# FFN gate and up projections as seven products of quadrants, with the down projection as a phase of its own

## The chip, the cores and the metric

One core of a Trainium2 chip runs the whole program. The time is device time in microseconds (us), lower is better. TensorE (PE) does the matmuls; VectorE (DVE), ScalarE (ACT) and GpSimd (POOL) do the element-wise work; SyncE (SP) issues the DMA transfers. Each engine works through its own list of instructions in a fixed order and waits where an operand is not there.

## The reference

The input is 1024 tokens of width 1024. Two attention layers (the first block) are followed by a second block, in which a SwiGLU feed-forward network stands at both ends of a mixing part:

```python
def swiglu(x, w_gate, w_up, w_down):
    return (jax.nn.silu(x @ w_gate) * (x @ w_up)) @ w_down
...
        h = h + 0.5 * swiglu(rms_norm(h, ffn1_norm[i]), ffn1_w_gate[i], ffn1_w_up[i], ffn1_w_down[i])
...
        h = h + 0.5 * swiglu(rms_norm(h, ffn2_norm[i]), ffn2_w_gate[i], ffn2_w_up[i], ffn2_w_down[i])
```

d_ff is 2816, so w_gate and w_up are 1024x2816 and w_down is 2816x1024. The mixing part between them has neighbourhood attention and an S5 state-space branch with a scan along the tokens; a small gated projection (ple) ends the program.

## The kernel before

All is fp32. Each fp32 operand is split into a high part and a remainder (hi, lo, both of type fp32r), and `mm3` forms a product with three matmuls per 128 rows of the contraction: hi with hi, hi with lo, lo with hi. So nearly everything on PE comes in threes, at lines 194, 195 and 196. Weights come from DRAM into a raw tile (`wraw`, two buffers), `split_w` makes hi on POOL (L184) and lo on DVE or POOL (L186).

The second block runs in this order: `ffn` (FFN1), `ssm_in` and `mix` (with the scan), `attn_out` and `mix_out`, `ffn` again (FFN2), `ple`. `ffn` goes through 22 tiles of 128 columns of d_ff. For one tile, `gate` and `up` each make two halves of 512 tokens (24 matmuls of 512 columns each, into PSUM tags G and S); tanh on ACT and products on DVE give the hidden tile, split again into hh and hl. For every two hidden tiles `down` multiplies with w_down (`draw`, split into dhi and dlo) and adds 16 pieces of 128x512 from PSUM tag T into h with DVE (L967). h, the residual, stays in SBUF. One FFN has 2112 gate and up matmuls and 1056 down matmuls, all of 512 columns.

In FFN1 the generator `also` is stepped once per tile; it is `ssm_matrices`, which makes the matrices of the scan with some 770 DVE operations on 64 columns (tiles gu, gM, gC; the rest of its tiles is called gen) and writes them to DRAM as `ssm_win`. The scan loads them as `sw` (L1183).

A tile framework fixes every engine's order at build time from the program's priorities; nothing is reordered on the chip.

## Time and profile before

| | |
|---|---|
| median of 3 runs | 3594.66 us (3594.66 to 3599.98) |
| the profiled execution | 3596.7 us |
| its span, first to last instruction | 3594.9 us |
| PE busy | 3463.1 us, 96% |
| DVE, ACT, POOL busy | 59%, 30%, 24% |
| mean granted TensorE clock | 0.987 |
| FFN1, FFN2 | about 1200 to 1955 us, about 2745 to 3465 us |

Busy time counts an instruction from its start to its end, and matmuls overlap their successors, so the pitch from start to start says what one costs. The granted clock is 1.00 at 2.4 GHz and 0.50 at 1.2 GHz; a stretch in between holds some of both. Windows are given in us from the span's start.

### The profile page before, as it was taken

What the parts mean: (1) busy time and instruction counts of PE and PEld (TensorE: products, weight loads), DVE (VectorE), ACT (ScalarE), POOL (GpSimd) and SP (SyncE); (2) the same over time, 40 slices, a digit from 0 to 9 for tenths busy, and PEclk for the clock granted to TensorE, in tenths of its full rate; (3) what the DMA queues carried; (4) which work ended last, traced back from release to release, by engine and by line L of the source; (5) the groups of instructions that cost most, each with busy time, mean ns of one, the idle gap of its engine ahead of it and who ended that gap; (6) DMA issues with size and microseconds to landing.
All of it is one profiled execution on the core that took longest, in us unless ns stands there. A gap on an engine that the chain in (4) does not pass through costs nothing. (4 is left out here: it accounts for less than half of the span.)

```text
span 3594.9 us, 53440 instructions
## 1 busy us (share of the span) xinstructions
PE 3463.1 (96%) x19400; PEld 3011.4 (84%) x19400; DVE 2108.4 (59%) x5436; ACT 1072.5 (30%) x2475; POOL 863.1 (24%) x970
## 2 busy tenths in 40 slices
PE   8999999999999999999999898998999999999998
PEld 7988899889889788888888786877798888888888
DVE  5656667646757966666544099428865444444465
ACT  3446645436745310000002310336611000000032
POOL 4233224323213311111112223343222101011112
PEclk9999999999999999999999999999999999999999
DMA  7567763657773222222212732577543111111113
GB/s 228 166 199 218 247 216 109 186 170 234 230 234 114 68 61 62 68 68 60 72 44 86 198 124 91 176 235 199 162 162 91 57 36 59 47 48 53 36 56 115
DMA packets 467671, 456.74 MB, mean 127 GB/s; under 512 B 45760, under 2 KB 354368, under 8 KB 467408
## 3 DMA queue, kind: packets, MB, share of 16 engines
q1 hardware_dynamic: 458192, 442.84, 40.9%
q10 hardware_dynamic: 9216, 10.49, 0.9%
q8 instruction: 154, 2.52, 0.3%
q14 instruction: 109, 0.89, 0.1%
HBM read 335.76 MB, written 117.41 MB: 126 GB/s over the span
## 5 line engine op out<-in xcount | busy, mean ns | idle before, releaser
L184 POOL TENSOR_SCALAR whi<-wraw 128x512 fp32r<-128x512 f32 (+1 forms) x460 | 297.3, 659 | 1903.1 <-PE G L195 837.9
L194 PE MATMUL G<-xh,whi 128*128 128x512 f32 x1472 | 583.9, 397 | 3.5 <-DVE slo L160 2.6
L196 PE MATMUL G<-xh,wlo 128*128 128x512 f32 x1472 | 578.6, 393 | 0.0
L195 PE MATMUL G<-xl,whi 128*128 128x512 f32 x1408 | 553.6, 393 | 0.2 <-DVE xl L157 0.2
L194 PE MATMUL G<-whi,xh 128*128 128x256 f32 (+1 forms) x1536 | 450.2, 293 | 10.2 <-DVE slo L157 5.8
L195 PE MATMUL G<-wlo,xh 128*128 128x256 f32 (+1 forms) x1536 | 444.2, 289 | 0.0
L967 DVE SCALAR_TENSOR_TENSOR h<-T,h 128x512 f32<-128x512 f32 x352 | 242.4, 689 | 333.8 <-PE T L196 331.5
L194 PEld LDWEIGHTS G<-xh,whi 128*128 128x128 f32 x1472 | 278.5, 189 | 62.3 <-DVE slo L160 2.9
L196 PEld LDWEIGHTS G<-xh,wlo 128*128 128x128 f32 x1472 | 277.9, 189 | 56.9
L195 PEld LDWEIGHTS G<-xl,whi 128*128 128x128 f32 x1408 | 266.3, 189 | 51.8 <-DVE xl L157 0.5
L194 PEld LDWEIGHTS G<-whi,xh 128*128 128x128 f32 x1536 | 296.7, 193 | 14.7 <-DVE slo L157 6.2
L195 PEld LDWEIGHTS G<-wlo,xh 128*128 128x128 f32 x1536 | 296.9, 193 | 1.0
L186 DVE TENSOR_TENSOR wlo<-wraw,whi 128x512 fp32r<-128x512 f32 x252 | 200.9, 811 | 118.4 <-POOL whi L184 118.3
L186 POOL TENSOR_TENSOR wlo<-wraw,whi 128x512 fp32r<-128x512 f32 (+1 forms) x208 | 267.8, 1301 | 4.7
L196 PE MATMUL G<-whi,xl 128*128 128x256 f32 (+1 forms) x896 | 262.8, 293 | 0.0
L194 PE MATMUL T<-dhi,hh 128*128 128x512 f32 x640 | 251.2, 393 | 0.0
L196 PE MATMUL T<-dhi,hl 128*128 128x512 f32 x640 | 249.4, 390 | 0.0
L195 PE MATMUL T<-dlo,hh 128*128 128x512 f32 x640 | 249.0, 389 | 0.0
L977 ACT ACTIVATE ft<-G 128x512 f32<-128x512 f32 x88 | 52.6, 597 | 579.9 <-PE G L196 579.8
L986 ACT ACTIVATE hh<-ft 128x512 fp32r<-128x512 f32 x88 | 54.5, 631 | 521.5 <-DVE ft L985 349.7
L194 PE MATMUL S<-xh,whi 128*128 128x512 f32 x512 | 200.2, 391 | 0.0
L196 PE MATMUL S<-xh,wlo 128*128 128x512 f32 x512 | 199.4, 390 | 0.0
(402 smaller groups left out, 7647.7 us busy)
## 6 DMA issues: line engine op xcount, KB each, us to landing
wraw<-w_in SPq DMA_DIRECT2D x144, 256.0 KB, 3.3
draw<-ffn_w_down SPq DMA_DIRECT2D x88, 256.0 KB, 2.6
wraw<-ffn_w_gate SPq DMA_DIRECT2D x86, 256.0 KB, 3.0
wraw<-ffn_w_up SPq DMA_DIRECT2D x86, 256.0 KB, 2.9
wraw<-w_out SPq DMA_DIRECT2D x64, 256.0 KB, 3.3
hk<-ka SPq DMA_DIRECT2D x48, 256.0 KB, 4.9
gs<-gt SPq DMA_DIRECT2D x32, 256.0 KB, 4.0
gl<-gs SPq DMA_DIRECT2D x32, 256.0 KB, 3.9
```

The source lines that it names most:

```text
L184: self.nc.gpsimd.tensor_scalar(hi, raw, 1.0, 0.0, op0=OP.mult, op1=OP.add)
L186: eng.tensor_tensor(lo, raw, f(hi), op=OP.subtract)
L194: t.matmul(out, lh, rh, start=first and i == 0, stop=False)
L195: t.matmul(out, lh, rl, start=False, stop=False)
L196: t.matmul(out, ll, rh, start=False, stop=last and i == n - 1)
L967: nc.vector.scalar_tensor_tensor(hs, ps, 0.25, hs, op0=OP.mult, op1=OP.add)
L977: nc.scalar.activation(t, pg, AF.Tanh, scale=0.5)
L986: nc.scalar.activation(hh[:, c], t, AF.Copy)
```

## The change

The activations x (tokens) and each weight are cut into quadrants. Instead of eight products of quadrants, seven products of sums are made (Strassen's scheme in Winograd's form): `ffn_up` takes 256 columns of gate or up at a time (11 steps, gate then up), and one product is 12 matmuls of 512 columns. The sums of x (s1 to s4) are made once in `halves_in` and `fourth`, mostly on POOL (L981, L983 and L989; these and the lines below are the changed kernel's); the sums of the weights (t1 to t4) are made on POOL (L1062 to L1065) for every step. `operand` splits each into hi (ACT) and lo (DVE, or POOL for w_down), in a ring of eight slots. The products are combined from PSUM on DVE (L1079 to L1092). The hidden tiles go to DRAM (`hid`, L1076).

`ffn_down` comes when all are done: for each half of the tokens and each half of the columns of w_down it accumulates four PSUM tiles over 22 steps k, 12 matmuls per step. In the first column half a hidden tile is loaded again (`hraw`, L1118) and split on ACT and DVE (L1120); w_down is loaded in both token halves. h comes from DRAM and goes there, in tiles hc and ht with two buffers each. `also` is stepped in this phase only, at every fourth k. Eight products (of j = 0 and 1) that need only the first half of the tokens are issued ahead of the rest.

Smaller edits: `weights` shifts tiles of 256 columns by 32 bytes; xn has one buffer in place of two; ple loads h from DRAM. Counted whole: 11 x 2 x 7 x 12 = 1848 gate and up matmuls per FFN in place of 2112, and 1056 down matmuls as before.

The core of the diff (the lines of `ffn` that go are in the listing above):

```diff
...
+    def weights(self, src, kt, n, pool=None, tag="w", bufs=4, raws=2, off=0):
+        o, size = off // 4, 1088 if pool is None else None
...
-            hi, lo = [self.T(pool, [128, 1088 if n == 352 else m * n], F32R, tag + x, bufs)[:, :m * n]
+            hi, lo = [self.T(pool, [128, size or m * n], F32R, tag + x, bufs)[:, o:o + m * n]
...
-        x = self.T(p, [128, 1024], F32, "xn", 2)
+        x = self.T(p, [128, 1024], F32, "xn", 1)
...
+    def halves_in(self, t, src, p, X, tag="T"):
...
+        sl = slice(t % 4 * 128, t % 4 * 128 + 128)
+        ps = []
+        for b in range(2):
+            ps.append(self.PS(tag, self.nT))
+            for j in range(4):
+                k = b * 4 + j
+                nc.tensor.transpose(ps[b][:, j * 128:j * 128 + 128], src[:, k * 128:k * 128 + 128], self.ident)
+            ps[b] = ps[b].rearrange("p (j n) -> p j n", j=4)
+        if t < 4:
+            hi, lo = X["a"]
+            for b in range(2):
+                self.split_ps(ps[b], hi[:, b * 4:b * 4 + 4, sl], lo[:, b * 4:b * 4 + 4, sl])
+            return
+        def tmp(n):
+            return self.T(p, [128, 4, 128], F32, n, 1)
+        def put(n, x):
+            hi, lo = [y[:, :, sl] for y in X[n]]
+            self.split_ps(x, hi, lo)
+        a21, a11, s1 = tmp("a21"), tmp("a11"), tmp("s1")
+        nc.scalar.activation(a21, ps[0], AF.Copy)
+        self.full(a11, X["a"], slice(0, 4), sl)
+        nc.vector.tensor_tensor(s1, ps[1], a21, op=OP.add)
+        put("b", ps[1])
+        put("s1", s1)
+        s2 = tmp("s2")
+        nc.gpsimd.tensor_tensor(s2, s1, a11, op=OP.subtract)
+        put("s2", s2)
+        nc.gpsimd.tensor_tensor(a21, a11, a21, op=OP.subtract)
+        put("s3", a21)
+        if "s4" in X:
+            self.fourth(sl, p, X, s2)
+    def full(self, dst, pair, k, sl):
+        self.nc.gpsimd.tensor_tensor(dst, f(pair[0])[:, k, sl], f(pair[1])[:, k, sl], op=OP.add)
+    def fourth(self, sl, p, X, s2=None):
+        a12 = self.T(p, [128, 4, 128], F32, "a11", 1)
+        self.full(a12, X["a"], slice(4, 8), sl)
+        if s2 is None:
+            s2 = self.T(p, [128, 4, 128], F32, "s2", 1)
+            self.full(s2, X["s2"], slice(0, 4), sl)
+        self.nc.vector.tensor_tensor(a12, a12, s2, op=OP.subtract)
+        hi, lo = [y[:, :, sl] for y in X["s4"]]
+        self.split_ps(a12, hi, lo)
+    def operand(self, src, lo_eng):
+        if not self.ring:
+            t = [self.T(self.wp, [128, 1024], F32R, x, 4) for x in ("whi", "wlo")]
+            self.ring = [[y[:, c:c + 512] for y in t] for c in (512, 0)]
+        hi, lo = self.ring.pop()
+        as_src = (lambda y: y.rearrange("p (k n) -> p k n", k=4)) if len(src.shape) == 3 else (lambda y: y)
+        self.nc.scalar.activation(as_src(hi), src, AF.Copy)
+        lo_eng.tensor_tensor(as_src(lo), src, as_src(f(hi)), op=OP.subtract)
+        return hi, lo
+    def ffn_up(self, X, wg, wu, hid, r, late, tags):
+        nc = self.nc
+        v = nc.vector
+        x = {n: [(hi[:, k], lo[:, k]) for k in range(4)] for n, (hi, lo) in X.items() if n != "a"}
+        x["a11"], x["a12"] = ([(X["a"][0][:, k], X["a"][1][:, k]) for k in range(b, b + 4)] for b in (0, 4))
+        turn = [0]
+        bufs = {"G": self.nG, "S": self.nS, "T": self.nT}
+        def product(W, n):
+            g = tags[turn[0] % len(tags)]
+            turn[0] += 1
+            ps = self.PS(g, bufs[g])
+            self.mm3(ps, self.four(W), x[n])
+            return ps
+        def tile(p, n, b):
+            return self.T(p, [128, 512], F32, n, b)
+        def first(w11, w21):
+            a = tile(r, "r1", 4)
+            nc.scalar.activation(a, product(w11(), "a11"), AF.Copy)
+            c = tile(r, "r2", 4)
+            v.tensor_tensor(c, a, product(w21(), "a12"), op=OP.add)
+            return a, c
+        def corner(src, j, k):
+            def get():
+                raw = self.T(self.wp, [128, 4, 128], F32, "wraw", 2)
+                nc.sync.dma_start(raw, src[k * 512:k * 512 + 512, j * 256:j * 256 + 128].rearrange("(k p) n -> p k n", p=128))
+                return self.operand(raw, v)
+            return get
+        early = {(j, i): first(corner(src, j, 0), corner(src, j, 1)) for j in range(2) for i, src in enumerate((wg, wu))}
+        p = late()
+        for j in range(11):
+            gates = {}
+            for i, src in enumerate((wg, wu)):
+                top, bot = [self.T(p, [128, 4, 256], F32, n, 2) for n in ("top", "bot")]
+                for k, y in enumerate((top, bot)):
+                    nc.sync.dma_start(y, src[k * 512:k * 512 + 512, j * 256:j * 256 + 256].rearrange("(k p) n -> p k n", p=128))
+                b11, b12, b21, b22 = top[:, :, 0:128], top[:, :, 128:256], bot[:, :, 0:128], bot[:, :, 128:256]
+                t1, t2, t3, t4 = [self.T(p, [128, 4, 128], F32, n, 1) for n in ("t1", "t2", "t3", "t4")]
+                if (j, i) in early:
+                    u, c11 = early[j, i]
+                else:
+                    u, c11 = first(lambda: self.operand(b11, v), lambda: self.operand(b21, v))
+                nc.gpsimd.tensor_tensor(t1, b12, b11, op=OP.subtract)
+                nc.gpsimd.tensor_tensor(t2, b22, t1, op=OP.subtract)
+                nc.gpsimd.tensor_tensor(t3, b22, b12, op=OP.subtract)
+                nc.gpsimd.tensor_tensor(t4, t2, b21, op=OP.subtract)
+                def done(c, hf, n):
+                    if i == 0:
+                        th = tile(p, "th", 2)
+                        nc.scalar.activation(th, c, AF.Tanh, scale=0.5)
+                        v.scalar_tensor_tensor(c, th, 1.0, c, op0=OP.add, op1=OP.mult)
+                        gates[hf, n] = c
+                    else:
+                        v.tensor_tensor(c, c, gates[hf, n], op=OP.mult)
+                        o = j * 256 + n * 128
+                        nc.sync.dma_start(hid[o:o + 128, hf * 512:hf * 512 + 512], c)
+                done(c11, 0, 0)
+                p6 = product(self.operand(t2, v), "s2")
+                v.tensor_tensor(u, u, p6, op=OP.add)
+                p7 = product(self.operand(t3, v), "s3")
+                u3 = tile(p, "r3", 2)
+                v.tensor_tensor(u3, u, p7, op=OP.add)
+                p5 = product(self.operand(t1, v), "s1")
+                c22 = tile(p, "r4", 2)
+                v.tensor_tensor(c22, u3, p5, op=OP.add)
+                v.tensor_tensor(u, u, p5, op=OP.add)
+                done(c22, 1, 1)
+                p3 = product(self.operand(b22, v), "s4")
+                v.tensor_tensor(u, u, p3, op=OP.add)
+                done(u, 0, 1)
+                p4 = product(self.operand(t4, v), "b")
+                v.tensor_tensor(u3, u3, p4, op=OP.subtract)
+                done(u3, 1, 0)
+    @staticmethod
+    def four(W):
+        return [(W[0][:, k * 128:k * 128 + 128], W[1][:, k * 128:k * 128 + 128]) for k in range(4)]
+    def ffn_down(self, hid, wd, src, dst, p, slots, then, also=None):
+        nc = self.nc
...
+        turn = 0
+        for hf in range(2):
+            H = slots(hf)
+            for c in range(2):
+                cs = slice(c * 512, c * 512 + 512)
+                acc = []
+                for t in range(4):
+                    g = "GS"[turn % 2]
+                    turn += 1
+                    acc.append(self.PS(g, self.nG if g == "G" else self.nS))
+                for k in range(22):
+                    hi, lo = H[k]
+                    if c == 0:
+                        raw = self.T(p, [128, 512], F32, "hraw", 3)
+                        nc.sync.dma_start(raw, hid[k * 128:k * 128 + 128, hf * 512:hf * 512 + 512])
+                        nc.scalar.activation(hi, raw, AF.Copy)
+                        nc.vector.tensor_tensor(lo, raw, f(hi), op=OP.subtract)
+                    raw = self.T(self.wp, [128, 512], F32, "wraw", 2)
+                    nc.sync.dma_start(raw, wd[k * 128:k * 128 + 128, cs])
+                    wh, wl = self.operand(raw, nc.gpsimd)
+                    for t in range(4):
+                        ts = slice(t * 128, t * 128 + 128)
+                        self.mm3(acc[t], [(hi[:, ts], lo[:, ts])], [(wh, wl)], k == 0, k == 21)
+                    if k % 4 == 3:
+                        next(also, None)
+                for t in range(4):
+                    rows = slice((hf * 4 + t) * 128, (hf * 4 + t) * 128 + 128)
+                    if c == 0:
+                        h = self.T(p, [128, 512], F32, "hc", 2)
+                        hc = h
+                    else:
+                        h = self.T(p, [128, 1024], F32, "ht", 2)
+                        nc.sync.dma_start(h[:, 0:512], dst[rows, 0:512])
+                        hc = h[:, cs]
+                    nc.sync.dma_start(hc, src[rows, cs])
+                    nc.vector.scalar_tensor_tensor(hc, acc[t], 0.25, hc, op0=OP.mult, op1=OP.add)
+                    nc.sync.dma_start(dst[rows, cs], hc)
+                    if c == 1:
+                        then(hf * 4 + t, h)
...
-            W = self.weights(self.I["w_out_2"][:, u * 256:u * 256 + 256], 8, 256)
+            W = self.weights(self.I["w_out_2"][:, u * 256:u * 256 + 256], 8, 256, off=32)
...
+                x = K.T(self.p, [128, 1024], F32, "xn", 1)
+                K.rms_tile(z, x, self.g)
+                K.halves_in(t, x, self.p, X)
...
+            def end(self):
+                self.X["s4"] = two(slot(K.big, "xl1"))
...
+                    K.fourth(slice(t * 128, t * 128 + 128), self.p, self.X)
...
+        self.ffn_up(nx.X, I["ffn1_w_gate_2"], I["ffn1_w_up_2"], hid, nx.r, late(nx.p, "late1"), "GSGSG")
...
+        self.ffn_down(hid, I["ffn1_w_down_2"], nx.hd, hd, p, places(nx.sx, p, ("xh0", "xl0"), ("xl1", "xh1"), ("sa", "sb", "sc"), 1), then, also())
...
+        self.ffn_up(X, I["ffn2_w_gate_2"], I["ffn2_w_up_2"], hid, r, late(p, "late2"), "GST")
...
+        self.ffn_down(hid, I["ffn2_w_down_2"], h2, h3, p, places(sx, p, ("xh0", "xh1"), ("xl0", "xl1"), ("sa", "sc", "sb")), then, also())
...
```

**At the entry of FFN1, PE.** Before, the last transposes of the normalized tokens (T<-ident) and what follows; the G and S rows are the first gate and up halves of the second 512 tokens.

```order
L195 MATMUL S_16548<-xl_3772_16072,whi_16452 128x512
L196 MATMUL S_16548<-xh_3771_16071,wlo_16453 128x512
L256 MATMUL T_16263<-ident,xn_16256 128x128 x4
L256 MATMUL T_16270<-ident,xn_16256 128x128 x4
L194 MATMUL G_16576<-xh_3793_16166,dhi_16386 128x512
L194 MATMUL S_16604<-xh_3793_16166,dhi_16396 128x512
L194 MATMUL G_16632<-xh_3793_16166,whi_16442 128x512
L194 MATMUL S_16660<-xh_3793_16166,whi_16452 128x512
```

After, at the same place; S_16561 is the first product that needs a sum of x (sb is the tile of s2) and a sum of weights.

```order
L196 MATMUL G_16524<-xh_3757_15875,whi_16501 128x512
L197 MATMUL G_16524<-sa_15876,whi_16501 128x512
L198 MATMUL G_16524<-xh_3757_15875,wlo_16502 128x512
L960 MATMUL T_16277<-ident,xn_16270 128x128 x4
L960 MATMUL T_16282<-ident,xn_16270 128x128 x4
L960 MATMUL T_16320<-ident,xn_16313 128x128 x4
L960 MATMUL T_16325<-ident,xn_16313 128x128 x4
L196 MATMUL S_16561<-sb_16178,whi_16557 128x512
L197 MATMUL S_16561<-sb_16178,whi_16557 128x512
L198 MATMUL S_16561<-sb_16178,wlo_16558 128x512
```

Before, products of plain weights follow the transposes; now a product of sums follows, and the ones of plain weights (G_16524) stand ahead of the transposes.

**At the same place, POOL.** Before: high parts of weights, and the layer norm and rstd of the last token tiles (h, rrs, lst).

```order
L539 TENSOR_TENSOR rrs_16138<-rrs_16138,mhalf 128x1
L690 TENSOR_TENSOR h<-h,lngb_14651 128x1024
L184 TENSOR_SCALAR whi_16452<-wraw_16454 128x512
L184 TENSOR_SCALAR whi_16452<-wraw_16458 128x512
L539 TENSOR_TENSOR rrs_16170<-rrs_16170,mhalf 128x1
L539 TENSOR_TENSOR lst_15940<-lst_15940,mhalf 128x1
L184 TENSOR_SCALAR whi_16819<-wraw_16821 128x512
L184 TENSOR_SCALAR whi_16819<-wraw_16825 128x512
L539 TENSOR_TENSOR rrs_16200<-rrs_16200,mhalf 128x1
L690 TENSOR_TENSOR h<-h,lngb_14651 128x1024
```

After, from the s2 of the last token tile to the sum t2 of the first weights:

```order
L981 TENSOR_TENSOR s_3840_16340<-s_3839_16332,a_3838_16331 128x512
L983 TENSOR_TENSOR a_3837_16330<-a_3838_16331,a_3837_16330 128x512
L989 TENSOR_TENSOR a_3842_16349<-xh_3757_15875,sa_15876 128x512
L989 TENSOR_TENSOR s_3843_16351<-sb_16178 128x512
L989 TENSOR_TENSOR s_3845_16358<-sb_16178 128x512
L989 TENSOR_TENSOR a_3844_16356<-xh_3757_15875,sa_15876 128x512
L989 TENSOR_TENSOR s_3847_16365<-sb_16178 128x512
L989 TENSOR_TENSOR a_3846_16363<-xh_3757_15875,sa_15876 128x512
L989 TENSOR_TENSOR s_3849_16372<-sb_16178 128x512
L989 TENSOR_TENSOR a_3848_16370<-xh_3757_15875,sa_15876 128x512
L1062 TENSOR_TENSOR t_3884_16546<-top_16542 128x512
L1063 TENSOR_TENSOR t_3885_16547<-bot_16543,t_3884_16546 128x512
```

Twelve additions of 128x512 stand between the last token tile and the first product of sums, where single high parts stood.

**In the middle of FFN1, DVE.** Before: gu, gM and gC are the scan's matrices; L967 adds into h, L985 makes the hidden tile, wlo is a low part of weights.

```order
L1046 TENSOR_TENSOR gu_3935_17274<-gM_17272,gen_16314 128x64
L967 SCALAR_TENSOR_TENSOR h<-T_17067,h 128x512
L1047 TENSOR_TENSOR gu_3936_17275<-gM_17272,gen_16315 128x64
L985 TENSOR_TENSOR ft_17196<-ft_17196,S_17227 128x512
L1048 TENSOR_TENSOR gM_17272<-gu_3935_17274,gu_3936_17275 128x4x16
L186 TENSOR_TENSOR wlo_17689<-wraw_17690,whi_17688 128x512
L1049 TENSOR_TENSOR gu_3935_17274<-gM_17272,gen_16314 128x64
L1050 TENSOR_TENSOR gu_3936_17275<-gM_17272,gen_16315 128x64
L186 TENSOR_TENSOR wlo_17689<-wraw_17694,whi_17688 128x512
L1051 TENSOR_TENSOR gM_17272<-gu_3935_17274,gu_3936_17275 128x4x16
```

After, in the down phase; hraw is a hidden tile that is loaded again, xl and so on its low part.

```order
L1173 TENSOR_TENSOR gM_20031<-gu_4491_20033,gu_4492_20034 128x4x16
L1120 TENSOR_TENSOR xl_4639_21298<-hraw_21331,xl_4639_21298 128x512
L1174 TENSOR_TENSOR gu_4491_20033<-gM_20031,gen_19750 128x64
L1175 TENSOR_TENSOR gu_4492_20034<-gM_20031,gen_19751 128x64
L1120 TENSOR_TENSOR xl_4639_21298<-hraw_21351,xl_4639_21298 128x512
L1176 TENSOR_TENSOR gM_20031<-gu_4491_20033,gu_4492_20034 128x4x16
L1171 TENSOR_TENSOR gu_4491_20033<-gM_20031,gen_19750 128x64
L1172 TENSOR_TENSOR gu_4492_20034<-gM_20031,gen_19751 128x64
L1120 TENSOR_TENSOR xl_4639_21298<-hraw_21373,xl_4639_21298 128x512
L1173 TENSOR_TENSOR gM_20031<-gu_4491_20033,gu_4492_20034 128x4x16
```

The same operations on matrices, which stood between all the FFN's other DVE work, now stand beside the hidden tiles of the down phase alone.

**From the products to the down phase, SP after the change.** The last stores of hidden tiles and the first loads.

```order
L1076 DMA hid_16377<-r_4425_19567 128x512
L1122 DMA wraw_19890<-ffn_w_down 128x512
L1076 DMA hid_16377<-r_4413_19475 128x512
L1076 DMA hid_16377<-r_4423_19550 128x512
L1122 DMA wraw_19944<-ffn_w_down 128x512
L1122 DMA wraw_19966<-ffn_w_down 128x512
L933 DMA rg_19615<-mix_norm 128x1024
L1118 DMA hraw_19635<-hid_16377 128x512
L1118 DMA hraw_19657<-hid_16377 128x512
L1118 DMA hraw_19677<-hid_16377 128x512
```

The first hidden tiles are loaded right behind the stores of the last ones; before the change there was no such place.

## Rows read from the trace of the kernel before

**Rows 1.** The page: busy time of each engine, share, instructions.

```profile
PE 3463.1 (96%) x19400; PEld 3011.4 (84%) x19400; DVE 2108.4 (59%) x5436; ACT 1072.5 (30%) x2475; POOL 863.1 (24%) x970
```

**Rows 2.** Windows of 600 us in FFN1 and FFN2.

```profile
core 0: us, PE busy (x) PEld busy (x) DVE busy (x) ACT busy (x) POOL busy (x), PEclk, DMA share, GB/s
1300.00:1900.00 600.00, 600.00 (x2725) 496.07 (x2724) 362.42 (x1010) 56.01 (x107) 74.54 (x122) 1.00 0.22 62
...
2800.00:3400.00 600.00, 600.00 (x2649) 496.81 (x2648) 254.62 (x368) 45.15 (x74) 69.36 (x110) 1.00 0.16 48
```

**Rows 3.** Timeline of PE in FFN1: start, duration; 116 pitches apart.

```profile
1889.67 0.39 PE L195 MATMUL T<-dlo,hh 128*128 128x512 f32 x1
...
1915.96 0.39 PE L194 MATMUL T<-dhi,hh 128*128 128x512 f32 x1
```

**Rows 4.** Timeline of PE: matmuls of 256 columns, 21 pitches apart.

```profile
1183.22 0.28 PE L196 MATMUL G<-whi,xh 128*128 128x256 f32 x1
...
1185.73 0.28 PE L196 MATMUL G<-whi,xh 128*128 128x256 f32 x1
```

**Rows 5.** The page: costly groups; busy us, mean ns, idle before.

```profile
L184 POOL TENSOR_SCALAR whi<-wraw 128x512 fp32r<-128x512 f32 (+1 forms) x460 | 297.3, 659 | 1903.1 <-PE G L195 837.9
...
L967 DVE SCALAR_TENSOR_TENSOR h<-T,h 128x512 f32<-128x512 f32 x352 | 242.4, 689 | 333.8 <-PE T L196 331.5
...
L186 DVE TENSOR_TENSOR wlo<-wraw,whi 128x512 fp32r<-128x512 f32 x252 | 200.9, 811 | 118.4 <-POOL whi L184 118.3
L186 POOL TENSOR_TENSOR wlo<-wraw,whi 128x512 fp32r<-128x512 f32 (+1 forms) x208 | 267.8, 1301 | 4.7
...
L986 ACT ACTIVATE hh<-ft 128x512 fp32r<-128x512 f32 x88 | 54.5, 631 | 521.5 <-DVE ft L985 349.7
```

**Rows 6.** Windows of 10 us at the entry of FFN1.

```profile
1170.00:1180.00 10.00, 8.72 (x74) 8.51 (x72) 9.89 (x21) 6.22 (x11) 5.97 (x5) 1.00 0.27 79
1180.00:1190.00 10.00, 6.71 (x49) 6.07 (x50) 10.00 (x23) 4.60 (x7) 6.81 (x6) 0.92 0.27 79
1190.00:1200.00 10.00, 10.00 (x36) 7.66 (x36) 9.50 (x18) 4.60 (x7) 7.07 (x8) 0.74 0.36 104
```

**Rows 7.** Timeline of PE after that wait: two 512-column matmuls.

```profile
1193.75 0.63 PE L194 MATMUL G<-xh,dhi 128*128 128x512 f32 x1
1194.18 0.63 PE L195 MATMUL G<-xl,dhi 128*128 128x512 f32 x1
```

**Rows 8.** DVE and POOL timelines during the scan, two answers.

```profile
2085.34 2.53 POOL L186 TENSOR_TENSOR wlo<-wraw,whi 128x512 fp32r<-128x512 f32 x2
...
2085.37 1.34 DVE L1205 TENSOR_TENSOR ssm_m<-ssm_x,l 128x64 f32<-128x64 f32 x1
2086.74 1.21 DVE L1206 TENSOR_TENSOR ssm_m<-ssm_m,ssm_m 128x64 f32<-128x64 f32 x1
...
2088.49 0.26 DVE L1205 TENSOR_TENSOR ssm_m<-ssm_x,l 128x64 f32<-128x64 f32 x1
```

**Rows 9.** Windows: DVE instructions that touch tile gu (matrices of the scan).

```profile
1200.00:1300.00 100.00, 24.88 (x119) 1.00 0.20 57
1300.00:1900.00 600.00, 135.28 (x649) 1.00 0.22 62
```

**Rows 10.** The page: DMA issues; KB each, us from issue to landing.

```profile
draw<-ffn_w_down SPq DMA_DIRECT2D x88, 256.0 KB, 2.6
...
hk<-ka SPq DMA_DIRECT2D x48, 256.0 KB, 4.9
```

**Rows 11.** Waits of PE from 1960 to 2310 us: total, times, longest.

```profile
PE T L1237 <- ACT se L1229: 18.6, 1, 18.6
PE S L1183 <- DMA sw<-ssm_win: 8.8, 1, 8.8
```

**Rows 12.** Window of 10 us after the scan.

```profile
2240.00:2250.00 10.00, 1.98 (x9) 1.96 (x10) 8.10 (x33) 2.64 (x5) 0.00 (x0) 0.50 0.00 0
```

**Rows 13.** Window of 10 us between FFN2 and ple.

```profile
3470.00:3480.00 10.00, 6.79 (x54) 6.16 (x52) 8.60 (x12) 4.47 (x8) 2.76 (x4) 0.94 0.42 135
```

More of the change, by code (lines that the diff above doesn't have):

```diff
@@ L1018, in ffn @@
         for _ in also:
             pass
-        down(pend, then)
     def exp_small(self, p, dst, src, shape):
@@ L1447, in ple_in, with ple @@
         return ph, pl
-    def ple(self, rp, pp, h, xT, out):
+    def ple(self, pp, hd, xT, out):
         nc, I = self.nc, self.I
         p = self.pool("ple", 1)
-        g = self.rms_gain(rp, I["final_norm_2"])
+        h = p.tile([128, 8, 1024], F32, name="h")
+        g = self.rms_gain(p, I["final_norm_2"])
+        for t in range(8):
+            nc.sync.dma_start(h[:, t], hd[t * 128:t * 128 + 128, :])
         x, ms = {}, {}
```

238 lines of the change are left out of this document (102 added, 136 removed).

## Prediction

> **What bounds the kernel now.** I read the page first: PE is busy 96% of the span and every other engine far less [rows 1], so the question is whether PE still works all the time in the two FFNs, which are what the change touches. The windows say yes: 600 us out of 600 in FFN1 and in FFN2, at full clock [rows 2]. There a removed matmul is worth its pitch, not its duration of 0.39 us, since matmuls overlap: 116 pitches take 26.29 us, so one of 512 columns costs 0.2267 us [rows 3]. DVE is at 60% in FFN1, POOL at 12%, DMA at 62 GB/s [rows 2]. That is the spare capacity that the change means to use. The places where PE does wait now are few: the entry of FFN1, where DVE is full [rows 6], the scan in the mixing part [rows 11], and the step into ple [rows 13].
>
> **What it removes.** 264 matmuls in each FFN, 528 in all, of 512 columns: 528 x 0.2267 = **-119.7 us**, if PE stays the bound wherever it was. In the product phase it does. One step of gate or up is 7 x 12 matmuls = 19.0 us of PE. DVE has seven low parts, seven or eight combinations and two or three closing operations for it, about 17 to 18 x 0.69 = 12 us [rows 5]; POOL four additions, bounded by the 1.30 us of its subtraction of equal size, 5.2 us; ACT seven high parts and up to four activations at 0.63, 7 us. All three have room and the operands come several products ahead, so I take nothing there. What hides these 12 us of DVE is PE's 19; without that cover the phase would follow DVE.
>
> **What it adds, place by place.**
>
> *Entry of FFN1.* Once the last tokens are transposed, a product of plain weights could run before; now the next product on PE needs s2 and t2, and twelve POOL additions stand in front of them in POOL's order: 12 x 1.30 = 15.6 us. Around them come a copy on ACT, s1 on DVE, then hi on ACT and lo on DVE: 2 x 0.63 + 2 x 0.69 = 2.6, so 18.2 us. Before, PE idles 1.3 + 3.3 = 4.6 us there [rows 6]; that makes 13.6 more. Each of the last four token tiles also brings five more DVE operations of 0.69 us, 13.8 us in all, to a DVE that is 95 to 100% busy [rows 6]. The eight products moved ahead cover part of that; I count half, 7. **+20** (10 if the products cover all the DVE work and part of the chain, 35 if nothing covers and the clock falls for longer).
>
> *From products to down phase, in each FFN.* PE's next matmul needs a hidden tile that has been to DRAM. In SP's order its load stands right behind the last stores, and those wait for DVE: two operations (1.4 us), the load (2.6, the nearest row of a 256 KB load) and ACT (0.6) make 4.6 us [rows 5, 10]. Then the clock: after the wait at FFN1's entry two matmuls of 512 columns are 0.43 us apart instead of 0.2267 [rows 7], and the clock reads 0.92 and 0.74 of two slices of 10 us, which is 0.8 + 2.6 = 3.4 us lost [rows 6]. **+16** for both (10 without the clock's part, 24 if the load also waits until the store has landed, for which 4.9 us is the longest row of that size [rows 10]).
>
> *Down phase of FFN1.* PE needs 1056 x 0.2267 = 239 us. Into this stretch the change puts all the scan's matrices, which were spread over 600 us. On DVE they are 768 operations and 160 us [rows 9]; 44 low parts of hidden tiles (30 us) and 16 additions into h (11 us) join them [rows 5]: 201 us, and nearly all the 64-column ones read two tiles in SBUF. POOL has 88 low parts of w_down there, 88 x 1.30 = 114 us. The timelines during the scan show what that does: while two such POOL operations run (2.53 us) DVE finishes two operations in 2.55, which alone take 0.26 or so each [rows 8]. One POOL operation thus costs DVE about 1.0 us, together 88 us: 201 + 88 = 289 us against PE's 239, **+50** if all matrices must be made in the phase. By the order the last two of eight sets of matrices stand behind the end, 40 us of the 160: then +10. PE is held up by this through the hidden tiles' low parts, which stand behind matrices in DVE's order, and through the matrices' own transposes on PE. Between the ends I take the middle, **+30**.
>
> *Changes of group in the down phase.* When four PSUM tiles are full they are read by DVE through tiles hc and ht, of two buffers each: one round is a load (2.6), DVE (0.7) and a store, and the next four accumulations need the banks. The order moves other steps in between, so I take 3 us for each of the three changes in FFN2, **+9** (0 to 20); in FFN1 they lie inside the 30.
>
> *Scan.* In the order before, the first matmuls on `sw` come eleven column groups of projection after FFN1; now thirteen. A group is 24 matmuls, 5.4 us, so the scan starts 10.9 us later, counted from FFN1's end, and PE already waits 18.6 us for its end and 8.8 us for its first matrices [rows 11]. What is late next is the output of the scan, T (L1237), and all of the mixing behind it. **+11** (0 if the wait for the matrices shrinks as much; 35 if the two late sets come on top).
>
> *Entry of FFN2 and step into ple.* The same chain as in FFN1, but there PE has more to do between the token tiles: +5 (0 to 15). ple now loads h and its first norm waits for the tiles ht; PE idles 3.2 us there already [rows 13]: +4 (0 to 10).
>
> *The rest at nothing.* w_down is read twice in all, 256 KB per 2.72 us with the hidden tiles' 256 KB beside it in half of the phase. One raw buffer goes load 2.6, ACT 0.63, POOL 1.30: 4.5 us, and there are two, so 2.3 us per step of 2.72; it fits, narrowly. The shift by 32 bytes concerns the operands of 256-column matmuls; they run at 21 pitches in 2.51 us, 0.12 each [rows 4], and no row shows an effect of the place. For about 4,200 of them each per cent would be 5 us, either way.
>
> **Sum.** -119.7 + 20 + 16 + 30 + 9 + 11 + 5 + 4 = **-25**. The profiled execution took 3596.7 us (3594.9 of it span), so 3572 there; the median lies 2 us lower, so **3570 us**. The lower ends of the terms add up to 30 and would give 3505, the upper ends to 189 and 3664; they will hardly meet.
>
> **Rivals.**
>
> *The gain is kept (3513).* DVE keeps up in the down phase because a quarter of the matrices is late anyway, and the order hides groups and scan. Then entry (20) and the two steps (16) are left: -119.7 + 36 = -84. For it: DVE's other work (L967, 352 x 689 ns [rows 5]) is gone. Against it: [rows 8].
>
> *FFN1's down phase decides, slower (3630).* If POOL and DVE strictly take turns, the phase needs POOL's 114 plus DVE's two-tile work, 160 + 30, which is 304 us: 64 over PE's 239 in place of 30, and the scan is 35 late in place of 11. Sum: +33, so 3628. It turns the result from 55 us over in that phase, since the other terms leave 55. For it speaks [rows 8]; against it that POOL's own mean, 1301 ns, hardly shows any waiting [rows 5].
> The Trainium skill (SBUF — State Buffer, "Who interferes with whom") has a rule for this: a DVE instruction with two SBUF inputs contends with a GpSimd instruction that reads SBUF, and whoever issues first keeps the port while the other stands still. The DVE side agrees with the rows on 1.34 against 0.26 us; the POOL side, that POOL waits as well, is not to be seen in its mean. By that side each low part of w_down could be 0.26 us late, the step 2.3 + 0.26 to 2.6 us, still under 2.72, so the sum would stay unless the loads are slower than 2.6.
>
> *Every step of the down phase waits a little, and the clock stays low (over 3640).* The ring for w_down has 0.4 us of room in 2.72. With loads of 4.9 us [rows 10] a step takes 3.4 us, and PE waits at each. After waits the clock is at its lower level, 0.50 [rows 12], and a step there takes 12 x 0.43 = 5.2 us [rows 7]. A third of 176 steps so would cost 59 x 2.4 = 142 us. Against it: loads of exactly this kind and size took 2.6 us at 62 GB/s, and now some 190 GB/s are wanted.
> The Trainium skill (TensorE: Matmul & The Clock Gate, "HAM oscillation") describes this pattern, a wait for DMA in each step of the contraction that makes the clock fall every time. The trace of before shows single falls after single waits, none that repeats; by the page's rule this rival's price would be right, without it the steps cost only the 0.7 us that they wait.
>
> **How the numbers follow.** My own case (3540 to 3600) has 0.50, the gain kept (3500 to 3540) 0.22, the decisive down phase 0.20, the low clock and other causes 0.08. I call the same what lies within 0.2% (7 us), about what a measurement of this kernel can tell. Of my own case 0.40 is faster, 0.08 the same and 0.02 slower; with the kept gain 0.62 is faster, and slower has 0.30 with the other two. The range for 8 in 10 runs from 3510, just under the rival that keeps the gain, to 3632, just above the decisive down phase; the own case's range is 3540 to 3600.
>
> **What would show it.** Right: PE 100% busy in the product phases, with 84 matmuls in 19.0 us; an idle stretch of 15 to 20 us at FFN1's entry ended by POOL; two of about 5 us ended by hraw; in FFN1's down phase DVE and POOL together near 100% and PE waiting for low parts of hraw or for matrices; a wait for the scan of 25 to 35 us. Wrong: a DVE that is not full in that phase, or PE waits that end on low parts of w_down or their loads, in both FFNs alike (then it is the ring); a product phase with PE below 98%; a different pitch at 256 columns.

## The result and the profile after

The changed kernel takes **3688.86 us** (median of 4, 3677.86 to 3696.21) against 3596.5 for the kernel before: ratio **1.0253** (1.0224 to 1.0282), slower. The forecast was 3570 with a range to 3632, so it was wrong in sign and the time lies outside. Of the rivals only the last, "over 3640", takes in the time, and its mechanism, a ring too slow in every step, is not what the trace shows (below); the decisive down phase (3630) is exceeded too. One of the four runs of the kernel h1 below, 3818 us at a clock of 0.85, is left out of its time.

The profiled execution has a span of 3690.2 us, 95.3 more than before [rows 1]. The page's first part, and the granted clock, which was 0.987:

```profile
PE 3393.3 (92%) x18872; PEld 2941.4 (80%) x18872; DVE 2302.4 (62%) x5508; ACT 1396.2 (38%) x3035; POOL 1249.0 (34%) x1094
```

```profile
core 0: 3690.2 us, clock 0.958
```

Two numbers split the 95.3. PE is idle for 3690.2 - 3393.3 = 296.9 us where it was idle for 131.8: 165.1 more. And its busy time fell by only 69.8 us although 528 matmuls (19400 to 18872, as counted) at 0.2267 us are gone, 119.7: the others took 50 us longer in all, at a mean clock of 0.958 in place of 0.987. -119.7 + 165.1 + 50 = 95.

Windows by stage: the entry of FFN1, its products, the step to the down phase, the down phase, and the last three again for FFN2 (columns as in [rows 2]):

```profile
1160.00:1260.00 100.00, 56.74 (x343) 49.52 (x342) 72.73 (x125) 46.85 (x79) 53.22 (x42) 0.77 0.24 79
1260.00:1657.00 397.00, 396.89 (x1747) 328.13 (x1746) 275.20 (x379) 120.22 (x209) 138.25 (x90) 1.00 0.27 83
1657.00:1668.00 11.00, 0.00 (x0) 0.00 (x0) 2.51 (x3) 1.56 (x3) 2.52 (x2) 0.69 0.75 244
1668.00:2010.00 342.00, 294.37 (x1296) 240.56 (x1296) 260.78 (x807) 97.84 (x182) 130.08 (x116) 0.91 0.49 151
2858.00:3258.00 400.00, 398.21 (x1748) 329.22 (x1748) 276.07 (x382) 121.19 (x210) 138.41 (x91) 0.99 0.27 85
3258.00:3271.00 13.00, 0.73 (x2) 0.64 (x3) 2.46 (x4) 1.97 (x4) 2.45 (x2) 0.66 0.79 248
3271.00:3550.00 279.00, 262.76 (x1134) 212.17 (x1132) 66.31 (x87) 86.59 (x146) 113.24 (x92) 0.95 0.48 152
```

The products behave as forecast, PE all but full at full clock for 400 us in both FFNs. The loss stands around them: 43 us idle at FFN1's entry, 48 in its down phase and 11 before it, 12 and 16 behind the products of FFN2, each with a clock below 1.00. FFN2's entry lost too. The first 100 us from its first transposes, after and then before:

```profile
2758.00:2858.00 100.00, 83.13 (x578) 76.26 (x576) 68.53 (x95) 35.15 (x64) 41.90 (x39) 0.90 0.35 116
```

```profile
2679.00:2779.00 100.00, 98.94 (x663) 90.64 (x662) 56.91 (x90) 20.42 (x37) 25.98 (x37) 1.00 0.30 93
```

In the first of them PE waits for a high part of weights and for xn:

```profile
PE T L196 <- ACT whi L1009: 8.3, 1, 8.3
PE T L960 <- DVE xn L947: 7.3, 3, 3.8
```

PE's waits at the entry of FFN1 (1150 to 1300 us) and in its down phase (1668 to 2010):

```profile
PE S L196 <- ACT whi L1009: 28.1, 1, 28.1
PE T L960 <- DVE xn L947: 14.9, 3, 6.9
```

```profile
PE O L1265 <- DVE gM L1173: 21.3, 6, 12.4
PE G L196 <- ACT xh L1119: 11.2, 1, 11.2
PE S L196 <- DVE hc L1139: 9.3, 2, 5.6
PE O L1273 <- ACT gW L1275: 7.0, 3, 3.3
PE T L258 <- DVE gM L1173: 6.0, 1, 6.0
```

At the entry there are two waits, and the second, for xn, was not in the forecast. In the second list the wait for xh is the step from the products (1657 to 1668 us), not the phase. In the phase itself (tag O is the scan's matrices) PE waits mostly for what DVE makes late, although DVE is busy for only 260.78 of the 342 us.

The first change of group in FFN2, where no matrices are in the way: DVE's additions into h, what SP does meanwhile, and PE.

```profile
3331.64 0.69 DVE L1139 SCALAR_TENSOR_TENSOR hc<-S,hc 128x512 f32<-128x512 f32 x1
3348.08 0.69 DVE L1139 SCALAR_TENSOR_TENSOR hc<-G,hc 128x512 f32<-128x512 f32 x1 [15.75 <-DMA hc<-h2d]
```

```profile
3323.72 17.70 SPq L1122 DMA_DIRECT2D wraw<-ffn_w_down  x8
3341.47 0.90 SPq L1140 DMA_DIRECT2D h3d<-hc  x2
```

```profile
3336.43 0.50 PE L197 MATMUL G<-wlo,xh 128*128 128x512 f32 x1 [0.85 <-POOL wlo L1010]
...
3338.48 0.50 PE L197 MATMUL G<-wlo,xh 128*128 128x512 f32 x1 [0.85 <-POOL wlo L1010]
...
3339.78 0.50 PE L196 MATMUL G<-whi,xh 128*128 128x512 f32 x1 [0.56 <-ACT whi L1009]
3341.12 0.79 PE L197 MATMUL G<-wlo,xh 128*128 128x512 f32 x1 [0.84 <-POOL wlo L1010]
...
3346.33 0.79 PE L197 MATMUL G<-wlo,xh 128*128 128x512 f32 x1 [0.55 <-POOL wlo L1010]
...
3350.27 0.63 PE L196 MATMUL G<-whi,xh 128*128 128x512 f32 x1
3350.70 0.63 PE L197 MATMUL G<-wlo,xh 128*128 128x512 f32 x1
```

The first hc is ready at 3332 and its store leaves at 3341, behind eight loads of weights that wait for their buffers; the third PSUM tile is read 16 us after the second. PE meanwhile works on one accumulator, three matmuls per step, and waits a little for each low part. After a few waits of less than 1 us its matmuls stand 0.43 us apart, as in [rows 7]. In windows of 10 us from 3330 to 3360 the change costs 6.5 us of idle time and 6.8 of clock:

```profile
3330.00:3340.00 10.00, 7.65 (x30) 1.00 0.40 115
3340.00:3350.00 10.00, 6.76 (x14) 0.53 0.62 192
3350.00:3360.00 10.00, 9.08 (x35) 0.79 0.64 219
```

One thing went better than put down. The three-pass matmuls of 256 columns, whose weights were shifted by 32 bytes, follow each other faster: 21 pitches take 2.52 us before and 2.46 after, at the same place.

```profile
149.65 0.28 PE L194 MATMUL G<-whi,xh 128*128 128x256 f32 x1
...
152.17 0.28 PE L194 MATMUL G<-whi,xh 128*128 128x256 f32 x1
```

```profile
148.99 0.29 PE L196 MATMUL G<-whi,xh 128*128 128x256 f32 x1
...
151.45 0.28 PE L196 MATMUL G<-whi,xh 128*128 128x256 f32 x1
```

Over the whole trace the mean pitch at full clock fell from 119.7 to 117.3 ns, and it is 117.3 to 117.5 in every kernel below; for 5159 such matmuls that is some 12 us of PE's work (an estimate from these figures). No run leaves the shift out, so neither its being the cause nor what reaches the span is shown.

### The profile page after: what moved, and what is told of

It is laid out like the page before. It is cut to its first block, busy times and chain, and to the rows that moved or that the text cites. A ratio compares the mean times of both kernels' runs of the same rounds, so it can differ in the third digit from the quotient of the medians.

```text
span 3690.2 us, 54259 instructions
## 1 busy us (share of the span) xinstructions
PE 3393.3 (92%) x18872; PEld 2941.4 (80%) x18872; DVE 2302.4 (62%) x5508; ACT 1396.2 (38%) x3035; POOL 1249.0 (34%) x1094
## 3 DMA queue, kind: packets, MB, share of 16 engines
q8 instruction: 150, 2.46, 0.3%
## 5 line engine op out<-in xcount | busy, mean ns | idle before, releaser
L196 PE MATMUL G<-whi,xh 128*128 128x256 f32 (+2 forms) x1472 | 441.3, 300 | 39.0 <-ACT xh L1119 24.1
L197 PE MATMUL G<-wlo,xh 128*128 128x256 f32 (+2 forms) x1472 | 434.7, 295 | 3.2 <-POOL wlo L1010 3.1
L197 PE MATMUL G<-xl,whi 128*128 128x512 f32 x1064 | 421.1, 396 | 0.2 <-DVE xl L158 0.2
L1010 POOL TENSOR_TENSOR wlo<-wraw,whi 128x512 fp32r<-128x512 f32 x176 | 234.1, 1336 | 347.8 <-ACT whi L1009 337.9
L198 PE MATMUL G<-whi,xl 128*128 128x256 f32 (+2 forms) x832 | 249.9, 300 | 0.0
L198 PE MATMUL G<-whi,xh 128*128 128x256 f32 (+1 forms) x832 | 246.1, 297 | 0.0
L158 DVE TENSOR_TENSOR ptl<-T,pth 128x512 fp32r<-128x512 f32 (+2 forms) x296 | 181.7, 629 | 20.3 <-ACT pth L157 16.8
L502 PE MATMUL T<-ident,P 128*128 128x128 f32 x1064 | 186.1, 279 | 7.3 <-DVE P L481 6.7
L157 ACT ACTIVATE pth<-T 128x512 fp32r<-128x512 f32 (+2 forms) x296 | 156.5, 553 | 54.9 <-PE T L502 50.8
L509 PE MATMUL O<-pth,hv 128*128 128x256 f32 (+1 forms) x616 | 166.3, 282 | 6.4 <-ACT pth L157 3.0
```

The source lines that it names most:

```text
L157: nc.scalar.activation(hi, ps, AF.Copy)
L158: nc.vector.tensor_tensor(lo, ps, f(hi), op=OP.subtract)
L196: t.matmul(out, lh, rh, start=first and i == 0, stop=False)
L197: t.matmul(out, lh, rl, start=False, stop=False)
L198: t.matmul(out, ll, rh, start=False, stop=last and i == n - 1)
L502: nc.tensor.transpose(ps[:, c + i * 128:c + i * 128 + 128], rows[bi][j], self.ident)
```

## The experiments

Stages are measured alike in all, from start to start: a down phase from the first hi part of a reloaded hidden tile to the last addition into h; between FFN1 and scan from that addition to the first matmul on `sw` (69.0 us before). The kernels e1 to e14 ran once each. In their traces and that of the change the attention ahead of FFN1 ends at 1151 to 1159 us, though its code is the same; so a few us of span say nothing, and the stages are compared.

| | FFN1's down phase | to the scan | FFN2's down phase | span |
|---|---|---|---|---|
| the change | 342.0 | 90.5 | 288.9 | 3690.2 |
| e1_thin | 327.1 | 71.0 | 291.3 | 3659.6 |
| e2_lodve | 303.1 | 104.0 | 279.6 | 3666.1 |
| e3_hc4 | 341.1 | 89.9 | 277.2 | 3686.2 |
| e4_entry | 344.5 | 89.5 | 291.5 | 3682.1 |
| e5_queue | 344.7 | 89.5 | 291.1 | 3687.5 |
| e6_nopieces | 340.3 | 69.0 | 291.0 | 3671.0 |
| e9_all | 304.7 | 101.8 | 266.3 | 3640.1 |
| e10_xn2 | 344.1 | 90.4 | 280.0 | 3681.1 |
| e11_gendve | 347.9 | 88.8 | 287.2 | 3694.0 |
| e12_lodve_thin | 294.4 | 72.2 | 275.2 | 3610.7 |
| e13_nomat | 303.3 | 69.2 | 292.1 | 3646.0 |
| e14_all_xn2 | 305.1 | 100.2 | 266.3 | 3625.3 |

In the expectations FFN2's phase is also called 279: that figure ends at 3550 us, ten before the last addition. In FFN1's phase PE is idle for 48 us in the change, 33 in e1, 16 in e2, 56 in e6, 28 in e13 and 11 in e12.

**Less arithmetic for the matrices** (each of two inner loops):

```diff
-self.cmul(M[:, 0, :, ms(k)], M[:, 1, :, ms(k)], ...)
+v.tensor_copy(M[:, :, :, ms(k)], M[:, :, :, ms(k - 1)])
```

> Two theories for FFN1's down phase, which took 342 us (1668 to 2010) where PE needs 239. A: DVE is the bound there, because the scan's matrices (768 operations on 64 columns) share it and each POOL low part holds them up. B: the SP queue is, because loads of w_down stand behind stores and loads that wait for something else. This kernel leaves out most of the matrices' arithmetic: their two inner loops copy instead of multiplying, 128 operations in place of 768, with the same transfers; its output is therefore not the reference's. A expects the phase at 280 us or less, like FFN2's down phase (279), no wait of PE for the matrices, and the whole at 3690 - 62 = 3628 or, with the scan's matrices earlier, 3615. B expects the phase above 320 us and the whole above 3665.

The phase fell by 15 us only, where A wanted 60; the way to the scan fell by 19.5, since the matrices were in time. The arithmetic alone isn't it.

**Low parts of w_down on DVE:**

```diff
-wh, wl = self.operand(raw, nc.gpsimd)
+wh, wl = self.operand(raw, nc.vector)
```

> The low parts of w_down go from POOL to DVE, 88 in each FFN. A expects that DVE's matrices run undisturbed: DVE then has 201 + 88 x 0.69 = 262 us of work where it had 289 with the blocked time, so FFN1's down phase falls by 20 to 30 us and the whole to about 3665. B expects no change there beyond 10 us. If the two raw buffers of w_down were the limit, FFN2's down phase would fall too, since a buffer comes free 0.6 us sooner; I expect it within 5 us of its 279.

39 us off FFN1's phase, more than A's 20 to 30, and 9 off FFN2's, where 5 at most was expected and no matrices are. One reason shows in the matrices' operations (DVE on tile gu, 1668 to 2010 us; the change, then this kernel):

```profile
1668.00:2010.00 342.00, 187.78 (x618) 0.91 0.49 151
```

```profile
1668.00:2010.00 342.00, 144.93 (x674) 0.94 0.51 159
```

187.78 / 618 = 304 ns each with POOL's low parts beside them, 215 without. The low parts themselves also come sooner, since DVE makes one in 0.69 us where POOL took 1.29 (medians); how the 39 us divide between the two isn't shown. And 14 of them came back: the matrices, later than the phase now, hold up the scan.

**More buffers for h in FFN2** (hc 2 to 4, ht 2 to 3):

> In FFN2's down phase alone the tiles of h have four and three buffers (hc, ht) in place of two. In the trace after, the store of the first hc leaves SP 9 us after it is ready, behind eight loads of w_down that wait for their buffers, and the third PSUM tile is read 16 us after the second. B expects the first change of group (13 us lost with the clock) to cost 3 us or less, FFN2's down phase to fall from 279 to about 262, the whole to about 3672. A says nothing of FFN2; if the changes cost what they cost because of PE's own order, the phase stays within 5 us.

The four additions now follow each other (3331.9, 3332.6, 3333.3, 3333.9) and the phase fell by 12, less than the 17 expected. But the first change of group still costs 12 us, 7.6 idle and 4.4 of clock:

```profile
3330.00:3340.00 10.00, 8.13 (x33) 5.55 (x31) 2.73 (x4) 3.16 (x5) 5.13 (x4) 1.00 0.36 106
3340.00:3350.00 10.00, 9.14 (x35) 7.18 (x36) 0.76 (x2) 1.81 (x4) 3.83 (x3) 0.83 0.71 229
3350.00:3360.00 10.00, 5.16 (x16) 3.67 (x15) 0.85 (x2) 0.77 (x2) 0.00 (x0) 0.73 0.69 244
```

PE still goes on with three matmuls per step, waits for low parts, and then 3.8 us for `pin`, a wait that had been hidden. So the late store was not what the first change cost; the gain came at the third change and at the end of the phase.

**The entry's order:**

```diff
 def end(self):
     self.X["s4"] = two(slot(K.big, "xl1"))
-    for t in range(4):
-        K.fourth(...)
...
 nc.gpsimd.tensor_tensor(t4, t2, b21, op=OP.subtract)
+(fourth() for the first four tiles, here)
```

> At FFN1's entry the sum s4 of the first four token tiles (eight POOL additions, four DVE subtractions and their split) comes after the first sums of weights, in tiles of the pool that the weights are in, so that this pool no longer waits for it. PE waits 28.1 us there in the kernel after. If POOL's chain is the cause, as the prediction said, it falls by 8 x 1.3 = 10 us; if also the load of the weights' lower half, which was issued only when the pool was free, at 1251, it falls to 10 us or less, and the whole by 18 to 22 us with the clock, to about 3670. If the wait has another cause it stays near 28.

The wait fell from 28.1 to 14.9 us. In the change the lower half of the weights was issued only at 1251, when the pool of xn was free, and POOL waited for it:

```profile
1248.06 1.26 POOL L1062 TENSOR_TENSOR t<-top 128x512 f32<-128x512 f32 x1
1255.13 1.26 POOL L1063 TENSOR_TENSOR t<-bot,t 128x512 f32<-128x512 f32 x1 [5.81 <-DMA bot<-ffn_w_gate]
```

The fall of 13.2 us is more than the 10 of POOL's chain and less than the 18 that both causes would have brought; the edit moves both, so their shares aren't shown. From the last matmul of attention to the first hi part of the down phase only 6 us were gained (510.3 to 504.3); another 6 of the span's 8 stand ahead of that stretch, in code that is the same.

**Transfers of h and of the matrices from ACT:**

```diff
-nc.sync.dma_start(hc, src[rows, cs])
+nc.scalar.dma_start(hc, src[rows, cs])
```

> Loads and stores of h in the down phases (hc, ht) and all transfers of the scan's matrices are issued by ACT in place of SP; nothing else changes. B (SP's queue holds up what stands behind a waiting transfer) expects the first change of group of FFN2 to fall from 13 us to 5 or less and FFN1's down phase from 342 us to 315 or less, the whole to about 3650. C, which the first four runs suggest (PE's own list is held up by the matrices' small matmuls, whose results the other engines' lists deliver late), expects FFN1's down phase to stay above 325. ACT's list may be held up in its turn.

Nothing: 344.7 and 291.1. In FFN2's first change the store of hc still leaves 6 us after it is ready (10 in the change), now behind ACT's high parts, the next load of hc leaves 6 us after that, and the third PSUM tile is again read 15 us after the second. A wait moved from one list into another, so this run alone does not rule B out; for FFN2's first change e3 says more.

**No matmuls, transposes and copies for the matrices:**

```diff
-nc.tensor.matmul(Gp[...], M[...], cb[...], ...)
-nc.tensor.transpose(ps[...], M[...], self.ident)
+nc.sync.dma_start(self.win_d[...], mf[...])
```

> The matrices' arithmetic on DVE stays whole, but their matmuls and transposes on PE (tag O), the copies on ACT (gen, gW) and on POOL behind them are left out; the results go to DRAM untransposed, so the scan works on other numbers. A (DVE's load with POOL's blocking) expects FFN1's down phase to stay near 330 us, as DVE has the same work. C expects about 300, FFN2's 289 and a few more: PE has no matmul left that waits for a matrix.

340.3, so C is out too, taken alone: 144 small instructions, some 15 us of PE's own work by their pitches (an estimate), left the list, and PE idles 8 us more. Its waits in the phase only changed their names:

```profile
PE G L196 <- ACT whi L1009: 20.7, 7, 8.4
PE T L258 <- DVE xn L947: 11.7, 3, 5.4
PE G L196 <- DVE gC L1173: 9.6, 1, 9.6
PE G L197 <- POOL wlo L1010: 8.3, 14, 0.9
```

**Copies into cb from POOL to DVE:**

```diff
-nc.gpsimd.tensor_copy(cb[es, :, :, e], cc[es])
+v.tensor_copy(cb[es, :, :, e], cc[es])
```

> Only the copies into cb (part of gen) go from POOL to DVE; w_down's low parts stay on POOL. In the kernel after POOL stands 28 us in FFN1's down phase at these copies, waiting for DVE, and low parts queue behind. If that is what moving the low parts to DVE cured (342 to 303 us), the phase falls to 315 or less here too. If it was POOL's blocking of DVE (A), the phase stays above 330, as POOL's low parts still run.

347.9: POOL's list was not what e2 cured.

**e2 and e1 together:**

> Low parts of w_down on DVE, and most of the matrices' arithmetic left out (copies in place of products, as in e1). A expects the two to be one cost: with POOL out of the way the arithmetic fits (201 + 61 us in 239 plus the waits between groups), so FFN1's down phase goes from 303 to 290 at most. If DVE's plain load is a cost of its own, it goes to FFN2's 280.

294.4, above both figures but nearer to A's 290, and the span falls by 55 us more than e2's, 32 of it on the way to the scan, since the matrices are no longer late. PE is nearly full in this phase, at a clock of 0.99:

```profile
1664.50:1958.90 294.40, 283.24 (x1344) 233.92 (x1344) 149.89 (x435) 101.03 (x192) 24.20 (x38) 0.99 0.60 183
```

**e1 and e6 together**, all of the matrices' work out:

> Both cuts at once, with w_down's low parts on POOL as in the change: most of the matrices' arithmetic is left out (e1) and so are their matmuls, transposes and copies (e6). Alone they brought FFN1's down phase from 342 to 327 and 340 us. If each of the two can hold the phase up by itself, it falls now to FFN2's 289, within 8 us, and the whole to about 3620. If POOL's low parts hold the phase up without the matrices, as in FFN1 the move to DVE brought 33 us even with the arithmetic cut, it stays above 310.

303.3, between the two figures expected (297 and 310). Alone the two brought 15 and 2, together 39: either is enough to hold most of the phase. Some 15 of the 39 are PE's own work, as in e6. What is left above FFN2's 292.1 in this kernel is 11 us.

**One or two buffers for xn.** First in the change, where SBUF has room:

```diff
-x = self.T(p, [128, 1024], F32, "xn", 1)
+x = self.T(p, [128, 1024], F32, "xn", 2)
```

> xn, the normed tile ahead of the transposes, has two buffers again at the entry of FFN2 and ahead of ple (at FFN1's two places there is no room in SBUF). In the kernel after, PE waits 7.1 us for xn at FFN2's entry and 11.5 us around ple. If the single buffer is the cause, both fall below 5 us and the stretch from FFN2's first transposes to the end, 931.7 us, falls by 10 to 20 us with the clock. If DVE's own pace is the cause, the waits stay.

The stretch from FFN2's first transposes to the end went from 931.7 to 912.6 us, and no wait for xn over 1 us is left there.

**FFN1 of before with FFN2 of the change**, improved, with one buffer for xn and then with two:

> The first block's end and FFN1 are those of before, so the scan's matrices stand in FFN1's single phase again; FFN2 is that of the change, with the low parts of w_down on DVE, four and three buffers for h and the new layout. In the kernel after, FFN2 from its first transposes to its last addition takes 800.7 us against 784.3 before; e2 and e3 took 9 and 12 off its down phase. If FFN2 is a matter of its own, the kernel takes 3596 + 16 - 21 - 4 = 3587; if the change's loss in FFN2 needs FFN1 too, the result lies elsewhere.

3629.13 us (median of three), ratio 1.0096 (1.0061 to 1.013). Of the 42 us above the 3587 expected, 29 were lost by the scan's start, behind an FFN1 that differs from before's in xn alone.

> The hybrid h1 (FFN1 of before, FFN2 of the change) with two buffers for xn everywhere and three and two for hc and ht. h1 lost 29 us by the start of the scan against before, where its FFN1 is the same but for xn: PE waited 22 us for xn at FFN1's entry, 12 at its end. If the single buffer is the cause, that comes back, and some 10 us in FFN2: 3630 - 29 - 10 = 3591, and faster than before by 5 us. If not, it stays at 3630.

3582.06, ratio **0.9942** (0.9923 to 0.9961), 0.6% faster than the kernel before. PE's wait at FFN1's entry, h1 and then h2:

```profile
PE T L258 <- DVE xn L947: 22.0, 3, 9.6
```

```profile
PE T L258 <- DVE xn L947: 3.0, 1, 3.0
```

> The hybrid with FFN2 as the change has it: low parts of w_down on POOL, two buffers for hc and ht, the change's layout; only xn has two buffers, as in h2. h2 took 0.9942 of before. e2 and e3 took 9 and 12 us off FFN2's down phase, so this kernel should take 15 to 20 us more than h2, 3600, and be no different from before. If it is as fast as h2, xn alone is what FFN2 needed.

0.9993 (0.9978 to 1.0008), no change, as expected. But the traces don't bear out the reason: of the 18 us between the spans of h2 and h3 (3585.0 and 3603.2) FFN2's down phase holds 6 (274.7 and 280.6), and 12 stand ahead of FFN2, in code that is the same. Nor is h2's gain shown to come from the seven products: from FFN2's first transposes to the end it takes 911.6 us against 915.1 before, and its 256-column matmuls are the faster ones, as in all these kernels. A kernel of before with the shift alone, the plain rival, was not run.

**All edits in the change itself:**

> Together: low parts of w_down on DVE, the entry's order, four and three buffers for h in FFN2, and the tiles of the down phase laid out so that the first reloaded hidden tiles lie where the weights' tiles were, not where the last sums were. If the gains add: 24 for the low parts, 9 for the entry, 12 for the buffers, 2 x 4 for the layout: 3690 - 53 = 3637, still slower than before. If all the waits are one chain that only moves, above 3655.

3641.91 (expected 3637), and with two buffers for xn:

> The kernel e9 (low parts on DVE, entry, layout, buffers) with two buffers for xn at FFN2's entry and ahead of ple, hc and ht three and two. e9 took 3642; e10 took 19 us off the stretch from FFN2's transposes to the end. If the gains add, 3623; still slower than before, by what FFN1 and the late matrices cost.

3627.09 (expected 3623). The gains add. From FFN2's first transposes to the end this kernel takes 900.3 us against 915.1 before; from the last matmul of attention to the scan it takes 46 more (908.8 against 862.7), and that keeps the whole above before.

## Why the prediction was wrong

The saving was right and so were most places of loss; the prices were not. By stage, before and after: from the last matmul of attention to FFN1's last addition 793.7 and 852.3 us, from there to the scan 69.0 and 90.5, from FFN2's first transposes to its last addition 783.6 and 800.0. With 59.9 us of matmuls gone from each FFN, FFN1 thus lost 118 us where 58 were forecast (20 + 8 + 30), and FFN2 76 where 22 were (5 + 8 + 9).

The table puts what each place added beside its term. The last column is an estimate: the time of the stage, less its matmuls at the pitches that they have at full clock in this trace, less the same in the kernel before.

| term | forecast | in the trace |
|---|---|---|
| entry of FFN1 | 20 | 38 |
| from products to down phase, both | 16 | 27 |
| down phase of FFN1 | 30 | 73 |
| down phase of FFN2 (changes of group) | 9 | 39 |
| scan | 11 | 22 |
| entry of FFN2 | 5 | 20 |
| step into ple | 4 | 0 |

- **What it removes** was right: 528 matmuls, and the product phases run at PE's pace.
- **Down phase of FFN1**, +30, is the largest miss, and the step that failed: it set DVE's total of work with POOL's blocking (289 us) against PE's 239 and read the loss from the difference. The phase took 342, of which about 30 are other PE work (240 small or projection matmuls and transposes) that stood in FFN1 before as well; 48 are idle time and about 25 slow matmuls. Yet DVE was busy for only 76% of it, which the prediction had named as a sign of being wrong, and with DVE busy for 41% (e1) the phase still took 327. So PE was not held up by DVE's total but by single results that come late in fixed orders (gM, hc and gW in the list of its waits). The two parts of the mechanism are real: moving POOL's low parts away takes 39 us off (e2), taking all the matrices' work out 39 too (e13), 15 of these PE's own. With both eased (e12) 21 of the 73 are left, and most of that phase is PE's own work. The stretching itself was overestimated (one matrix operation went from 215 to 304 ns, 68 us over 768, not 88).
- **Changes of group**, +9 in FFN2, are some 26 of the 39, by their slices of 10 us. The text priced a round of load, addition and store at 3 us. The first change alone took 13, half of it clock, and still 12 when the round was gone (e3): PE runs ahead of the low parts on one accumulator, at three matmuls per step, which the text did not see. e3 and e2 took 12 and 9 off the phase, both with the layout (e9) 22.6; PE then idles 8 of 266 us, so little is left.
- **Entry of FFN1**, +20, was too small. POOL's chain was there (28.1 where 18.2 was worked out; the load of the weights came late as well), but the single buffer of xn was at nothing, as the text did not price it: 14.9 us of waits here. In FFN1 of before, h1 and h2, which differ in xn (and in a buffer each for hc and ht), are 47 us apart.
- **Entry of FFN2**, +5, has the same two waits, 8.3 and 7.3 us; there and ahead of ple the second buffer for xn brings 19 us (e10).
- **From products to down phase**: the load of the first hidden tile took 5.4 and 7.4 us from issue to landing, where 2.6 were priced; from the last closing operation to the first hi part it was 8 and 10 us (1659.3 to 1667.4, 3259.7 to 3269.6), and PE waited 11.2 and 12.9 where 4.6 were worked out.
- **Scan**, +11, was 22: the late matrices (e1 and e6 bring the stretch back to 71 and 69) rather than two more column groups.
- **The sum**: the text took the clock in two terms of 3.4 us each. Here the slower matmuls cost some 50 us, a third of what the idle time cost.
- **The shift by 32 bytes**, at nothing, came with a pitch 2% shorter at 256 columns, a sign that the text had named; it works against the loss.

The Trainium skill (TensorE: Matmul & The Clock Gate, "HAM oscillation") has the pattern that the low-clock rival was built on, waits in each step that bring the clock down every time. The trace agrees in part: not in the steady steps, where the clock reads 1.00, but after each change of group of FFN2, where slices of 10 us read 0.53 to 0.83. The rival named the right range, over 3640, for another reason: PE's waits for w_down's low parts and high parts in FFN2's phase come to 6 us, and they stand at the changes.

The rival "the gain is kept" failed on the same rows. "FFN1's down phase decides" had the right place and nearly the right price: 64 and 35 for the scan, where 73 and 22 came. What took the time beyond its 3628 lies in the two entries, the steps and FFN2's changes of group.

Open: through which of PE's waits matrices and POOL's low parts hold FFN1's phase up together, as each cut moved the wait elsewhere; and what the shift of the 256-column operands brings alone.

## What to carry to other kernels

Fewer matmuls are worth their pitch only while nothing else in their stage becomes a chain; a phase that is cut out of an interleaved loop brings its own entry, changes and end, and each idle spot on PE should be priced with the slow matmuls behind it. Price every edit that gives up a buffer: here one tile of 4 KB per partition was worth about 47 us, over twice what h2 gains on the kernel before. Compare stages and not spans where code that is the same varies by some us. Work that used to be spread over 600 us (the scan's matrices) needs its own place when its host shrinks to 240.

## What was not expected of the hardware

The clock fell without a long wait: at FFN2's first change of group PE waited 0.85, 0.85, 0.56 and 0.84 us between 3335 and 3341, with matmuls in between, and then its matmuls stood 0.43 us apart. And DVE's copies with one source in SBUF were stretched beside POOL's operations as well, 369 ns on average in e1 against 230 in e12 (L1249, gM, 128x128):

```profile
L1249 DVE COPY gM<-gM 128x128 f32<-128x128 f32 x56 | 20.6, 369 | 1.2
```

```profile
L1249 DVE COPY gM<-gM 128x128 f32<-128x128 f32 x56 | 12.9, 230 | 1.3
```

In one kernel POOL makes the low parts of w_down, in the other DVE does.
